# A hybrid DeltaNet / SSD decoder step: GpSimd's work between the projections moved to VectorE and ScalarE

## The chip, the cores and the metric

The kernel runs on one core of a Trainium2 chip. A core has TensorE (PE, matrix products, results in PSUM), VectorE (DVE), ScalarE (ACT), GpSimd (POOL) and SyncE (SP, which here only issues transfers). Each engine works through its own list of instructions in order and waits on semaphores for the others. The metric is the device time of one execution in microseconds; 1% of it is 28 us.

## The reference

One step of a decoder layer, for a prompt of 512 tokens and for 8 samples of 8 tokens each that continue from a state; the 576 rows are worked on together. Cut to what matters:

```
proj = rmsnorm(x) @ w_in                       # 2048 -> 6688
q, k, v = silu(causal_conv(...)); beta, g, dt from small columns
# gated delta rule, 8 heads, chunks of 64 in the reference:
low = strict(kb @ k.T * decay);  sol = solve(low + I, [v*beta, kb*exp(G)])
step: v_new = u - w @ S;  o = q_dec @ S + qk @ v_new;  S = S*g_last + k_dec.T @ v_new
o = rmsnorm(o) * silu(z)
# SSD, 2 groups of 8 heads:
step: y = (C B^T * decay) @ xdt + C_dec @ h;   h = h*a_last + (B*decay).T @ xdt
y = rmsnorm((y + D*x) * silu(z))
x = x + concat(o, y) @ w_out
x = x + (silu(rmsnorm(x) @ w_gate) * (rmsnorm(x) @ w_up)) @ w_down
y = rmsnorm(x)
```

The outputs are y for prompt and samples and the new convolution and matrix states. All of it is float32: each large product is split into a high and a low part of weights and activations and done as three matmuls.

## The kernel before, in words

There are three parts. The first (up to about 580 us) does the norm, most of the input projection and the convolutions, and leaves its results in memory (cvd, zd, gad). The third (from about 1183 us) is the rest of the output projection (`out_proj`, L1329) and the feed-forward part. The change lies in the second part, between the projections.

The second part has two kinds of work. The **chains** are `ssd(g, sd)` for two groups and `gdn(h, G)` for eight heads; each is a long line of small products, evictions and elementwise steps. A head works on four chunks of 128 columns: it builds a triangular matrix u, inverts it in blocks (16 by substitution on VectorE in t16, t16m, with a trip through memory, then 32, 64 and 128 by matmuls with the block masks bm), and then goes through the chunks (`prompt`), the samples (`sample`), the norm (`norm`) and the sample states (`states`). Heads have two sets of buffers (`slot`), so two heads are under way together. Group 0 and group 1 of the SSD run beside heads 0 to 3; each ends with a sample part that loads, scales and stores 8 states (st8, in `big`).

The **filler** are the gate projections not yet done (`gates`) and half of the output projection (`half_out`). Their matmuls write the bank pz; all other matmuls of the part write banks pm0 to pm5 (pm_5552 to pm_5557 in the order of instructions; pm_5552 and pm_5553 belong to even heads, pm_5554 and pm_5555 to odd ones). Their weights are split by ScalarE (whi) and VectorE (wlo) in pieces of 256 columns.

The order of the second part is not that of the code. The operations are noted first (L116 is the line at which a noted operation is issued, so nearly all rows of the part carry L116), with an engine, a price and what each depends on. Then `in_order` lays them out: a list scheduler that takes, over all engines, the operation that can start first by these prices, and among those the one with the longest way to the end behind it; filler matmuls come last among equals. Prices are by engine, in microseconds for n columns: VectorE's 0.07 + n / 940 for most operations, ScalarE's 0.06 or 0.085 + n / 1170, and for GpSimd

```
NPOOL = Noted("pool", nc.gpsimd, lambda op, n, ins: 0.13 + n / (300 if op == "tensor_copy" else 600))
```

The prices know nothing of one engine holding another, nor of TensorE's clock. The result is one fixed list per engine. So a change of the engine of an operation changes the order of everything behind it on all engines of this part. The third part is in an order written by hand.

GpSimd does in the second part: in `ssd` the products xdec, bex and st8 by the decay, the sum zacc and the copies eal; in `gdn` the copies egl and t16, the products of kd, q and S, the clear of ubd and the products ubd and um with the block masks.

Of the kernel before, what the change touches and what calls it, by code (L numbers as in the profile page):

```python
# [15 lines left out]
P = 128  # L16
NP = 512
NS = 64
NT = NP + NS
# [19 lines left out]
def build(tc, I, O):  # L39
    nc = tc.nc  # L40
    PE, DVE, ACT, POOL, SP = nc.tensor, nc.vector, nc.scalar, nc.gpsimd, nc.sync
    act = ACT.activation
    tt, ts, stt = DVE.tensor_tensor, DVE.tensor_scalar, DVE.scalar_tensor_tensor
    mult, add, sub, amin = ALU.mult, ALU.add, ALU.subtract, ALU.min
    with ExitStack() as ctx:
# [721 lines left out]
        def ssd(g, sd):  # L767
# [12 lines left out]
            for c in range(4):  # L780
                cc = slice(c * P, (c + 1) * P)
                for half in range(2):
                    SP.dma_start(out=ab[half], in_=gad[r0 + 4 * half:r0 + 4 * half + 4, cc].partition_broadcast(P))
                px = sbank()
                for q in range(4):
                    PE.transpose(px[:, q * P:(q + 1) * P], xs[:, q, cc], ident)
                tt(h8(xdt), h8(px), sct[:, c, 64 + 8 * g:72 + 8 * g].unsqueeze(2).broadcast_to([P, 8, 64]), mult)
                POOL.tensor_tensor(h8(xdec), h8(xdt), edl[:, c, r0:r0 + 8].unsqueeze(2).broadcast_to([P, 8, 64]), mult)
                pc = sbank()
                PE.matmul(pc[:, 0:P], bt[:, cc], ct[:, cc], start=True, stop=True)  # L790
                stt(cb, neg, 0.0, pc[:, 0:P], op0=ALU.is_ge, op1=mult)
                py = banks[5]
                for half in range(2):
                    h0 = r0 + 4 * half
                    a, d = ab[half], dec[half]
                    for j in range(4):
                        ts(d[:, j, :], a[:, j, :], sct[:, c, h0 + j:h0 + j + 1], 0.0, op0=sub, op1=amin)
                    act(d, d, AF.Exp)
                    act(a, a, AF.Exp)
                    tt(d, d, cb.unsqueeze(1).broadcast_to([P, 4, P]), mult)  # L800
                    POOL.tensor_copy(eal[:, 4 * half:4 * half + 4], a[:, :, P - 1])
                    if c:
                        tt(a, a, ct[:, cc].unsqueeze(1).broadcast_to([P, 4, P]), mult)
                    for q in range(2):
                        pr = 2 * half + q
                        for step in range(2 if c else 1):
                            for s in range(2):
                                hh, j = 2 * pr + s, 2 * q + s
                                o = py[64 * s:64 * s + 64, pr * P:(pr + 1) * P]
                                if step == 0:  # L810
                                    PE.matmul(o, h8(xdt)[:, hh, :], d[:, j, :], start=True, stop=not c)
                                else:
                                    PE.matmul(o, h8(hst)[:, hh, :], a[:, j, :], start=False, stop=True)
                pn = sbank()
                PE.matmul(pn, btok4[:, c, :], xdec, start=True, stop=True)
                for q in range(4):
                    stt(xs[:, q, cc], xs[:, q, cc], dpair[:, 4 * g + q:4 * g + q + 1], py[:, q * P:(q + 1) * P], op0=mult, op1=add)
                    new = hsts[c % 2]
                if c:
                    tt(h8(new), h8(hst), eal.unsqueeze(2).broadcast_to([P, 8, 64]), mult)  # L820
                    tt(new, new, pn, add)
                else:
                    ACT.copy(new, pn)
                hst = new
# [10 lines left out]
            for q in range(4):  # L835
                PE.transpose(px[:NS, q * P:(q + 1) * P], xs[:, q, sl], ident)
            tt(h8(xdt)[:NS], h8(px)[:NS], sct[:NS, 4, 64 + 8 * g:72 + 8 * g].unsqueeze(2).broadcast_to([NS, 8, 64]), mult)
            POOL.tensor_tensor(h8(xdec)[:NS], h8(xdt)[:NS], edl[:NS, 4, r0:r0 + 8].unsqueeze(2).broadcast_to([NS, 8, 64]), mult)
            pc = dbank()
            PE.transpose(pc[:NS, 0:P], bt[:, sl], ident)  # L840
            PE.matmul(pc[:NS, P:P + NS], bt[:, sl], ct[:, sl], start=True, stop=True)
# [1 line left out]
            ACT.copy(cbs, pc[:NS, P:P + NS])  # L843
            ACT.copy(bts, pc[:NS, 0:P])
            bex = bb[:NS, 0:8 * P].rearrange("p (a b) -> p a b", a=8)
            POOL.tensor_tensor(bex, bts.unsqueeze(1).broadcast_to([NS, 8, P]), bmask.unsqueeze(2).broadcast_to([NS, 8, P]), mult)
            ds = dec[0].rearrange("p a b -> p (a b)")[:NS].rearrange("p (a b) -> p a b", a=8)
            SP.dma_start(out=ds, in_=gad[r0:r0 + 8, sl].partition_broadcast(NS))
            for s in range(2):
# [13 lines left out]
            for q in range(4):  # L863
# [8 lines left out]
                po = dbank()  # L872
                for b in range(8):
                    PE.matmul(po[:, 8 * b:8 * b + 8], (ab[0], dec[0])[b // 4][:, b % 4, :], ct[:, NP + 8 * b:NP + 8 * b + 8], start=True, stop=True)
                POOL.tensor_tensor(st8, st8, ep[:, q, 7::8].unsqueeze(2).broadcast_to([P, 8, P]), mult)
                tt(yo, po[:, 0:NS], ep[:, q, :], mult)
                tt(xs[:, q, sl], xs[:, q, sl], yo, add)
                for half in range(2):
# [7 lines left out]
            for q in range(4):  # L886
                t = (zt, ct)[q % 2]
                SP.dma_start(out=t, in_=zd[8 + 4 * g + q])
                tt(xs[:, q], xs[:, q], t, mult)
                if q == 0:  # L890
                    act(zacc, xs[:, q], AF.Square)
                else:
                    act(t, xs[:, q], AF.Square)
                    POOL.tensor_tensor(zacc, zacc, t, add)
            ps = dbank()
            for i in range(5):
                n = P if i < 4 else NS
# [75 lines left out]
        def gdn(h, G):  # L973
# [35 lines left out]
            act(u, u, AF.Exp)  # L1009
            act(us, us, AF.Exp)  # L1010
            act(g, g, AF.Exp)
            POOL.tensor_copy(egl[:, 0:4], g[:, P - 1:NP:P])
            POOL.tensor_copy(egl[:, 4:12], g[:, NP + 7:NT:8])

            pq, pv = bank(), bank()
            for c in R4:
# [10 lines left out]
            PE.transpose(pkts[:, 0:NS], kds, ident[:NS, :NS])  # L1027
            ACT.copy(kt[:, 0:NP], pkt)
            ACT.copy(kt[:, sl], pkts[:, 0:NS])
            POOL.tensor_tensor(v4(kd), v4(kd), edl[:, 0:4, h:h + 1].broadcast_to([P, 4, P]), mult)  # L1030
            ts(kds, kds, edl[:NS, 4, h:h + 1], None, op0=mult)

            pkk, paq = bank(), bank()
# [14 lines left out]
            SP.dma_start(out=dap(ud, 0, [[P, P], [UC, 4], [1, P]]), in_=v4(u))  # L1048
            SP.dma_start(out=dap(ud, 4 * UC, [[P, NS], [1, NS]]), in_=us)
            SP.dma_start(out=u16[0:36], in_=dap(ud, 0, [[UC // 8, 36], [P, 16], [1, 16]]))  # L1050
            POOL.tensor_copy(t16, id16)
            ts(eq, eq, EPS, EPS * P, op0=add, op1=mult)
            tt(kq[:, :, 0:8], b8(kt[:, sl]), b8(g[:, sl]), mult)
            tt(kq[:, :, 8:16], b8(q[:, sl]), b8(g[:, sl]), mult)
            tt(kt[:, 0:NP], kt[:, 0:NP], g[:, 0:NP], mult)
            POOL.tensor_tensor(q[:, 0:NP], q[:, 0:NP], g[:, 0:NP], mult)
            ubd, xbd, um = (aw[:, i, 0:n].rearrange("p (a b) -> p a b", b=P) for i, n in ((0, 640), (1, 640), (2, 512)))
            POOL.memset(ubd[:, 4, :], 0.0)
            POOL.tensor_tensor(ubd[:, 0:4, :], v4(u), flat2(bm[:, 0]).unsqueeze(1).broadcast_to([P, 4, P]), mult)
            DVE.tensor_copy(ubd[:NS, 4, 0:NS], us)  # L1060
            POOL.tensor_tensor(um, v4(u), flat2(bm[:, 1]).unsqueeze(1).broadcast_to([P, 4, P]), mult)
            for i in range(15):
                m, w = 15 - i, i + 1
                pr = t16m[:36, 0:m * w].rearrange("p (a b) -> p a b", b=w)
# [73 lines left out]
            def sample():  # L1138
# [2 lines left out]
                for i in range(8):  # L1141
                    PE.matmul(pr[:, 16 * i:16 * i + 16], S[:, i, :], kq[:, i, :], start=True, stop=True)
                ACT.copy(ksq.rearrange("p a (b t) -> p b a t", t=8), pr[:, 0:P].rearrange("p (b a t) -> p b a t", a=2, t=8))
                POOL.tensor_tensor(S, S, egl[:, 4:12].unsqueeze(2).broadcast_to([P, 8, P]), mult)
                pr = bank()
                PE.transpose(pr[:NS, 0:P], ksq[:, 0, :], ident)
                tt(rs, vps, pr[:NS, 0:P], sub)
# [548 lines left out]
```

## Time and profile before

| | us |
|---|---|
| median of 3 runs | 2792.08 |
| the runs | 2801.77, 2778.82, 2792.08 |
| profiled execution, its own time | 2805.85 |
| its span, first to last instruction | 2804.1 |
| mean granted TensorE clock | 0.973 |

The page of the profile gives for each engine the busy time and its share of the span. A clock of 1.00 is TensorE's full 2.4 GHz, 0.50 is 1.2 GHz; the figure for a stretch is the mean over it. A row of the order of time gives the start, the duration, the engine, the line, the operation with what it writes and reads, its shape, and in brackets how long the engine had stood idle before it and what ended that. An instruction's duration runs from its start to its end, also where it was held in between. Matmuls overlap in part, so their durations don't add up to time. Names are those of the buffers, so that, for instance, `aw` is k, v, g, later ubd, xbd, um and S of a head, `big` holds the sample states of the SSD, and `cf` the unit matrix of a transpose.

### The profile page before, as it was taken

Reading aid. Unit: us, or ns where it says so; the run is one execution under the profiler, and the core shown is the slowest. Engines: PE = TensorE matmul, PEld = TensorE weight load, DVE = VectorE, ACT = ScalarE, POOL = GpSimd, SP = SyncE. Lnnn points to the kernel's source line nnn. Section 1 sums busy time; section 2 is a strip of 40 time slices with the busy share of each in tenths; the row PEclk is TensorE's granted clock in tenths of the full one; section 3 lists DMA queues with packets and bytes.
Section 4 is the critical chain, followed back from the end, with each engine's and each line's share of the span. In section 5 each row is a group of like instructions: output and inputs, shape, how many; then the busy total and the mean of one; then the engine's idle time right before and its main releaser. Section 6 shows DMA issues by size and latency. Waiting matters only on the chain.

```text
span 2804.1 us, 49909 instructions
## 1 busy us (share of the span) xinstructions
PE 2686.4 (96%) x19535; PEld 2583.4 (92%) x19535; DVE 2135.1 (76%) x3275; ACT 1284.7 (46%) x2441; POOL 604.0 (22%) x584
## 2 busy tenths in 40 slices
PE   7999999988998999999999999999999989999897
PEld 5999999977868898899999999999999989999896
DVE  5977888866668767588777777777777787887686
ACT  6544455542424533364443434343343455555465
POOL 1111111113122111032111010101111143343264
PEclk9999999997879999999999999999999999999999
DMA  4444444363445545464343444434343477787643
GB/s 114 118 121 116 124 124 116 114 180 107 142 128 164 170 117 151 136 196 113 98 129 109 131 115 118 128 98 128 105 132 110 137 178 191 178 189 174 161 128 133
DMA packets 580138, 380.03 MB, mean 136 GB/s; under 512 B 37022, under 2 KB 545115, under 8 KB 579326
## 3 DMA queue, kind: packets, MB, share of 16 engines
q1 hardware_dynamic: 546606, 328.91, 41.5%
q0 software_dynamic: 8384, 20.06, 4.1%
q10 hardware_dynamic: 24912, 27.88, 3.3%
q8 instruction: 153, 2.51, 0.4%
q14 instruction: 83, 0.68, 0.1%
HBM read 290.34 MB, written 86.42 MB: 134 GB/s over the span
## 4 chain that ended last, share of the span: by engine, by line
PE 52%; DVE 6%; DMA 3%; ACT 2%; issue 2%; POOL 0%; ACTq 0%; SPq 0%; DVEq 0%; POOLq 0%
PE pF L284 45%; PE pz L116 3%; PE pm L116 2%; PE pA L1329 1%; DMA wraw<-w_up 1%; DVE wlo L275 1%; DMA wraw<-w_down 1%; ACT whi L269 1%; DVE X L1301 1%; DVE ws L257 0%; DVE ws L265 0%; DMA wraw<-w_out 0%; ACT sc L1366 0%; DVE sc L1379 0%; DVE wlo L116 0%
## 5 line engine op out<-in xcount | busy, mean ns | idle before, releaser
L284 PE MATMUL pF<-X,whi 128*128 128x288 f32 x7350 | 1477.2, 297 | 25.4 <-ACT sc L1366 14.8
L284 PEld LDWEIGHTS pF<-X,whi 128*128 128x128 f32 x7350 | 1182.1, 189 | 32.9 <-ACT sc L1366 17.7
L284 PE MATMUL pF<-X,wlo 128*128 128x288 f32 x3675 | 1085.3, 295 | 0.7 <-DVE wlo L275 0.7
L284 PEld LDWEIGHTS pF<-X,wlo 128*128 128x128 f32 x3675 | 693.4, 189 | 1.6 <-DVE wlo L275 1.6
L116 PE MATMUL pF<-XR,whi 128*128 128x288 f32 (+1 forms) x2560 | 491.5, 298 | 0.6 <-DVE XR L116 0.5
L116 PEld LDWEIGHTS pF<-XR,whi 128*128 128x128 f32 (+1 forms) x2560 | 399.7, 189 | 2.6 <-DVE XR L116 1.0
L275 DVE TENSOR_TENSOR wlo<-wraw,whi 128x1024 fp32r<-128x1024 f32 (+5 forms) x285 | 355.3, 1247 | 14.4 <-ACT whi L269 13.9
L269 ACT CAST whi<-wraw 128x1024 fp32r<-128x1024 f32 (+5 forms) x285 | 266.7, 936 | 190.4 <-DVE wraw L262 66.9
L116 PE MATMUL pF<-XR,wlo 128*128 128x288 f32 (+1 forms) x1280 | 337.3, 298 | 4.0 <-DVE wlo L116 4.0
L116 ACT CAST whi<-wraw 128x256 fp32r<-128x256 f32 (+2 forms) x241 | 153.5, 643 | 270.1 <-PE pz L116 156.7
L116 PE MATMUL pz<-XR,whi 128*128 128x288 f32 x1184 | 267.7, 328 | 8.1 <-ACT zo L116 4.5
L1368 DVE TENSOR_TENSOR sc<-pF,sc 128x288 f32<-128x288 f32 x231 | 105.3, 456 | 221.8 <-PE pF L284 221.5
L269 ACT CAST whi<-ws 128x1024 fp32r<-128x1024 f32 (+5 forms) x153 | 141.4, 924 | 243.5 <-DVE ws L257 154.4
L116 PEld LDWEIGHTS pF<-XR,wlo 128*128 128x128 f32 (+1 forms) x1280 | 227.2, 189 | 5.0 <-DVE wlo L116 4.5
L116 DVE TENSOR_TENSOR wlo<-wraw,whi 128x256 fp32r<-128x256 f32 (+2 forms) x241 | 175.5, 738 | 59.9 <-PE pz L116 31.8
L116 PEld LDWEIGHTS pz<-XR,whi 128*128 128x128 f32 x1184 | 193.8, 202 | 24.2 <-issue 11.3
L1386 POOL TENSOR_TENSOR sc<-sc 128x288 f32<-128x288 f32 x22 | 37.2, 1689 | 802.6 <-DVE sc L1383 802.6
L269 ACT CAST whi<-sc 128x1024 fp32r<-128x1024 f32 (+5 forms) x101 | 89.7, 888 | 257.7 <-DVE sc L254 246.0
L1301 POOL TENSOR_TENSOR X<-X 128x288 fp32r<-128x288 f32 x140 | 146.0, 1051 | 204.3 <-ACT X L1300 176.2
L275 DVE TENSOR_TENSOR wlo<-ws,whi 128x1024 fp32r<-128x1024 f32 (+5 forms) x153 | 173.0, 1131 | 20.2 <-ACT whi L269 17.2
L1366 ACT COPY sc<-pF 128x288 f32<-128x288 f32 x308 | 121.8, 395 | 116.8 <-PE pF L284 100.5
L116 PE MATMUL pz<-XR,wlo 128*128 128x288 f32 x592 | 152.9, 327 | 0.0
(372 smaller groups left out, 3570.2 us busy)
## 6 DMA issues: line engine op xcount, KB each, us to landing
wraw<-w_in SPq DMA_DIRECT2D x104, 512.0 KB
wraw<-w_gate SPq DMA_DIRECT2D x88, 512.0 KB
wraw<-w_up SPq DMA_DIRECT2D x88, 512.0 KB
ffd<-sc SPq DMA_DIRECT2D x154, 144.0 KB
X<-ffd ACTq DMA_DIRECT2D x154, 144.0 KB
wraw<-w_down SPq DMA_DIRECT2D x45, 384.0 KB
yd<-sc POOLq DMA_DIRECT2D x26, 576.0 KB, 6.5
wraw<-w_out SPq DMA_DIRECT2D x22, 512.0 KB
```

The source lines that it names most:

```text
L116: note("dma" if op == "dma_start" else self.name, price, lambda: f(*a, **k), outs, ins, kind, op == "matmul" and not (k["start"] and k["st ...
L269: ACT.copy(hi, r)
L275: tt(lo, r, hi.bitcast(F32), sub)
L284: PE.matmul(o, a[:, k, :], b, start=k == 0 and r == 0 and q not in CHAINED, stop=k == n - 1 and r == 2, skip_group_check=q in CHAINED)
L1301: e.tensor_tensor(X[t][s][:, 1, :], raw, X[t][s][:, 0, :].bitcast(F32), sub)
L1329: PE.matmul(ps[:, l, 0:HT], w[:, kk], b[:, k, l * HT:l * HT + HT], start=k == k0 and q == 0, stop=k == 7 and q == 2)
L1366: ACT.copy(b, o)
L1368: tt(b, o, b, add)
L1386: POOL.tensor_tensor(t1, b12, b11, sub)
```

## The change

Fifteen lines in `ssd` and `gdn` name another engine. Products, sums and the clear go to VectorE (`tt` is VectorE's tensor_tensor), copies to ScalarE. Nothing else of the code changes, neither prices nor shapes. GpSimd then has nothing to do in the second part; it keeps its work in the first and third.

```diff
@@ -785,7 +785,7 @@
-                POOL.tensor_tensor(h8(xdec), h8(xdt), edl[:, c, r0:r0 + 8].unsqueeze(2).broadcast_to([P, 8, 64]), mult)
+                tt(h8(xdec), h8(xdt), edl[:, c, r0:r0 + 8].unsqueeze(2).broadcast_to([P, 8, 64]), mult)
@@ -798,7 +798,7 @@
-                    POOL.tensor_copy(eal[:, 4 * half:4 * half + 4], a[:, :, P - 1])
+                    ACT.copy(eal[:, 4 * half:4 * half + 4], a[:, :, P - 1])
@@ -835,7 +835,7 @@
-            POOL.tensor_tensor(h8(xdec)[:NS], h8(xdt)[:NS], edl[:NS, 4, r0:r0 + 8].unsqueeze(2).broadcast_to([NS, 8, 64]), mult)
+            tt(h8(xdec)[:NS], h8(xdt)[:NS], edl[:NS, 4, r0:r0 + 8].unsqueeze(2).broadcast_to([NS, 8, 64]), mult)
@@ -843,7 +843,7 @@
-            POOL.tensor_tensor(bex, bts.unsqueeze(1).broadcast_to([NS, 8, P]), bmask.unsqueeze(2).broadcast_to([NS, 8, P]), mult)
+            tt(bex, bts.unsqueeze(1).broadcast_to([NS, 8, P]), bmask.unsqueeze(2).broadcast_to([NS, 8, P]), mult)
@@ -872,7 +872,7 @@
-                POOL.tensor_tensor(st8, st8, ep[:, q, 7::8].unsqueeze(2).broadcast_to([P, 8, P]), mult)
+                tt(st8, st8, ep[:, q, 7::8].unsqueeze(2).broadcast_to([P, 8, P]), mult)
@@ -891,7 +891,7 @@
-                    POOL.tensor_tensor(zacc, zacc, t, add)
+                    tt(zacc, zacc, t, add)
@@ -1009,8 +1009,8 @@
-            POOL.tensor_copy(egl[:, 0:4], g[:, P - 1:NP:P])
-            POOL.tensor_copy(egl[:, 4:12], g[:, NP + 7:NT:8])
+            ACT.copy(egl[:, 0:4], g[:, P - 1:NP:P])
+            ACT.copy(egl[:, 4:12], g[:, NP + 7:NT:8])
@@ -1027,7 +1027,7 @@
-            POOL.tensor_tensor(v4(kd), v4(kd), edl[:, 0:4, h:h + 1].broadcast_to([P, 4, P]), mult)
+            tt(v4(kd), v4(kd), edl[:, 0:4, h:h + 1].broadcast_to([P, 4, P]), mult)
@@ -1048,17 +1048,17 @@
-            POOL.tensor_copy(t16, id16)
+            ACT.copy(t16, id16)
 ...
-            POOL.tensor_tensor(q[:, 0:NP], q[:, 0:NP], g[:, 0:NP], mult)
+            tt(q[:, 0:NP], q[:, 0:NP], g[:, 0:NP], mult)
 ...
-            POOL.memset(ubd[:, 4, :], 0.0)
-            POOL.tensor_tensor(ubd[:, 0:4, :], v4(u), flat2(bm[:, 0]).unsqueeze(1).broadcast_to([P, 4, P]), mult)
+            DVE.memset(ubd[:, 4, :], 0.0)
+            tt(ubd[:, 0:4, :], v4(u), flat2(bm[:, 0]).unsqueeze(1).broadcast_to([P, 4, P]), mult)
 ...
-            POOL.tensor_tensor(um, v4(u), flat2(bm[:, 1]).unsqueeze(1).broadcast_to([P, 4, P]), mult)
+            tt(um, v4(u), flat2(bm[:, 1]).unsqueeze(1).broadcast_to([P, 4, P]), mult)
@@ -1141,7 +1141,7 @@
-                POOL.tensor_tensor(S, S, egl[:, 4:12].unsqueeze(2).broadcast_to([P, 8, P]), mult)
+                tt(S, S, egl[:, 4:12].unsqueeze(2).broadcast_to([P, 8, P]), mult)
```

Since the orderer works with other engines and prices, the lists of all engines change in this part. Two places, as the lists stand before and after.

VectorE, in the middle of the third head (names with 5589 to 5610 are the even heads' buffers), before:

```order
L116 TENSOR_TENSOR at_5595<-pm_5553,u_5594 128x512
L116 TENSOR_SCALAR rk_5633<-rk_5633 128x5
L116 TENSOR_TENSOR kq_5610<-q_5591,aw_5589 128x8x8
L116 TENSOR_TENSOR ty_5637<-rk_5633 128x5
L116 SCALAR_TENSOR_TENSOR u_5594<-pm_5552,u_5594 128x512
L116 SCALAR_TENSOR_TENSOR ty_5637<-ty_5637,tx_5636 128x5
L116 TENSOR_TENSOR kt_5592<-kt_5592,aw_5589 128x512
```

and after:

```order
L116 TENSOR_TENSOR at_5595<-pm_5553,u_5594 128x512
L116 TENSOR_TENSOR q_5591<-q_5591,aw_5589 128x512
L116 SCALAR_TENSOR_TENSOR u_5594<-pm_5552,u_5594 128x512
L116 TENSOR_TENSOR kt_5592<-kt_5592,aw_5589 128x512
L116 TENSOR_TENSOR wlo<-wraw,whi 128x256
L116 TENSOR_TENSOR XR_94<-xs,XR_93 128x576
L116 TENSOR_TENSOR ats_5600<-pm_5552,us_5599 64x64
L116 COPY kds_5625<-pm_5555 64x128
L116 SCALAR_TENSOR_TENSOR us_5599<-pm_5552,us_5599 64x64
L116 TENSOR_TENSOR aw_5589<-u_5594,bm 128x512
L116 COPY aw_5589<-us_5599 64x64
L116 TENSOR_TENSOR aw_5589<-u_5594,bm 128x512
```

The product of q now stands between the products at and u, and the two products with the block masks stand behind the last step of us; before, these three were in GpSimd's list.

TensorE, at the end of the second part (pA is the first product of the output projection's rest), before:

```order
L116 MATMUL pm_5554<-at_5623,kds_5625 128x512
L116 MATMUL pz<-XR_93,whi 128x288
L116 MATMUL pz<-XR_94,whi 128x288 x2
L116 MATMUL pz<-XR_93,wlo 128x288 x2
...
L116 MATMUL pz<-XR_89,whi 128x288 x2
L116 MATMUL pz<-XR_88,wlo 128x288 x2
L1329 MATMUL pA<-XR_88,whi 128x288 x2
```

and after, from the last filler on:

```order
L116 MATMUL pz<-XR_88,wlo 128x288 x2
L116 MATMUL pm_5554<-vp_5624,u_5622 128x128
L116 MATMUL pm_5553<-bw_5590,kt_5592 128x128
L116 MATMUL pm_5555<-bw_5618,kd_5621 128x128
L116 MATMUL pm_5554<-bw_5618,at_5623 128x128
...
L116 MATMUL pm_5552<-at_5595,kds_5597 128x512
L116 MATMUL pm_5555<-at_5623,kds_5625 128x512
L116 MATMUL pm_5554<-at_5623,kds_5625 128x512
L1329 MATMUL pA<-XR_88,whi 128x288 x2
```

Before, fillers stand between the chains' last matmuls and behind them (167 behind the product of vp and u of the last head). After, the last filler stands just ahead of that product, and the 65 matmuls from it to the last state product follow one another with none between. The number of fillers in the part, 1776, is the same.

## Rows read from the trace of the kernel before

**Rows 1.** The page: busy time by engine; the chain that ended last.

```profile
PE 2686.4 (96%) x19535; PEld 2583.4 (92%) x19535; DVE 2135.1 (76%) x3275; ACT 1284.7 (46%) x2441; POOL 604.0 (22%) x584
...
PE 52%; DVE 6%; DMA 3%; ACT 2%; issue 2%; POOL 0%; ACTq 0%; SPq 0%; DVEq 0%; POOLq 0%
```

**Rows 2.** Busy time by stretch: length, engines' busy us (instructions), granted clock, DMA share, GB/s.

```profile
640.00:730.00 90.00, 83.68 (x403) 71.92 (x404) 53.33 (x165) 26.15 (x60) 23.96 (x21) 0.66 0.42 112
...
670.00:680.00 10.00, 10.00 (x30) 7.18 (x30) 4.92 (x27) 0.81 (x2) 0.00 (x0) 0.50 0.59 160
...
770.00:830.00 60.00, 56.37 (x288) 41.13 (x289) 38.58 (x109) 15.49 (x40) 12.99 (x11) 0.70 0.41 115
...
580.00:1190.00 610.00, 564.31 (x3811) 485.75 (x3809) 416.05 (x1285) 236.10 (x735) 113.01 (x114) 0.90 0.50 143
```

**Rows 3.** GpSimd's groups by shape, 600 to 1200: count, busy us, mean ns, idle before.

```profile
L116 POOL TENSOR_TENSOR aw<-u,bm 128x512 f32<-128x512 f32 x16 | 23.1, 1449 | 11.2 <-DVE u L116 4.2 <-DVE bts L116 2.3 <-DVE wlo L116 1.1
...
L116 POOL COPY eal<-big 128x4 f32<-128x4 f32 x7 | 3.2, 452 | 10.3 <-ACT big L116 10.3
```

**Rows 4.** VectorE's and ScalarE's nearest groups by shape, 600 to 1200.

```profile
L116 DVE TENSOR_TENSOR at<-bw,bmask 64x512 f32<-64x512 f32 x16 | 11.8, 742 | 7.2 <-PE pm L116 4.4 <-ACT bw L116 2.7
...
L116 DVE TENSOR_TENSOR big<-big,cb 128x512 f32<-128x512 f32 x7 | 4.8, 683 | 0.0
...
L116 DVE TENSOR_TENSOR xs<-xs,zt 128x576 f32<-128x576 f32 x4 | 3.0, 748 | 0.0
...
L1324 DVE TENSOR_TENSOR wlo<-wraw,whi 128x1024 fp32r<-128x1024 f32 x2 | 2.4, 1218 | 2.0 <-ACT whi L1323 2.0
...
L116 ACT COPY u<-pm 64x256 f32<-64x256 f32 x8 | 2.9, 367 | 4.6 <-DVE u L116 4.5
```

**Rows 5.** Order of time, VectorE beside GpSimd: start, us, engine, line, operation.

```profile
586.08 1.68 DVE L116 TENSOR_SCALAR dec<-ab,scr 128x128 f32<-128x128 f32 x4
...
665.92 1.91 POOL L116 TENSOR_TENSOR big<-big,zt 128x1024 f32<-128x1024 f32 x1 [3.90 <-PE pm L116]
666.01 1.89 DVE L116 TENSOR_TENSOR t16m<-u,t 36x63 f32<-36x63 f32 x1
...
667.94 0.22 DVE L116 TENSOR_TENSOR t<-t,t16m 36x63 f32<-36x63 f32 x1
...
1157.36 1.66 DVE L116 TENSOR_TENSOR at<-bw,bmask 64x512 f32<-64x512 f32 x1 [1.98 <-ACT bw L116]
```

**Rows 6.** Order of time, TensorE's gaps that VectorE ends.

```profile
588.69 2.05 PE L116 MATMUL pm<-xdec,bb 128*128 128x512 f32 x2 [1.99 <-DVE cb L116]
...
639.64 1.23 POOL L116 TENSOR_TENSOR kd<-kd,scr 128x512 f32<-128x512 f32 x1
639.88 1.06 DVE L116 TENSOR_SCALAR kds<-kds,rk 64x128 f32<-64x128 f32 x1
...
641.00 0.27 PE L116 MATMUL pm<-cf,kds 64*128 64x64 f32 x1 [1.51 <-DVE kds L116]
...
1092.81 0.24 PE L116 MATMUL pm<-cf,kds 64*128 64x64 f32 x1 [0.54 <-DVE kds L116]
```

**Rows 7.** Order of time at the end of the second part.

```profile
1137.45 0.38 PE L116 MATMUL pm<-vp,u 128*128 128x128 f32 x2
...
1171.47 0.32 SPq L116 DMA_DIRECT2D mixd<-z  x1
...
1173.55 0.43 SPq L116 DMA_DIRECT2D xs<-mixd  x1
...
1181.20 0.69 PE L116 MATMUL pz<-XR,whi 128*128 128x288 f32 x4
...
1181.40 0.76 DVE L116 TENSOR_TENSOR XR<-xs,XR 128x576 fp32r<-128x576 f32 x1
...
1181.73 0.43 PE L116 MATMUL pz<-XR,wlo 128*128 128x288 f32 x2
...
1183.09 0.77 PE L1329 MATMUL pA<-XR,whi 128*128 128x288 f32 x4 [0.94 <-DVE xs L116]
```

## The prediction

> **What bounds the kernel now.** I read the page first: its line of engine shares and its chain that ended last [rows 1]. TensorE is busy for 96% of the span, and over half of the chain that ended last is TensorE; GpSimd stands in that chain with 0%. So GpSimd sets the time only through others. Next I read the table of stretches [rows 2]. The change touches only the middle part between the two projections, which fills the window from 580 to 1190 us, 610 us of a span of 2804.1. There TensorE is busy for 564.31 us, so it idles for 45.7, and its granted clock is 0.90 of full. The clock is the larger loss: 0.10 x 610 is some 61 us. Of it 0.34 x 90 = 31 us fall between 640 and 730, and 0.30 x 60 = 18 us between 770 and 830; from 900 on the clock is 1.00. A stretch at 0.50 is the lower of the two levels, 1.2 GHz. VectorE is busy for 416 of these 610 us (68%), GpSimd for 113.
>
> Then the operations by shape, GpSimd's [rows 3] and their nearest on VectorE and ScalarE [rows 4]. A 128x512 product takes 1.45 us on GpSimd and 0.68 on VectorE; a copy of four columns takes 0.45 on GpSimd.
>
> Then the order of time where GpSimd and VectorE meet [rows 5]. At 665.92 GpSimd starts a product of 1.91 us. At 666.01 VectorE starts a 36x63 product; it takes 1.89 us, and the next one of that size takes 0.22. VectorE stood until GpSimd was through. I went through all VectorE rows of the window: 54 of them are more than 0.1 us longer than the lower quartile of their own group while GpSimd is busy, the first at 586.08 and the last at 1157.36, and what is over sums to 52.6 us.
>
> Last, TensorE's waits [rows 6]. At 641.00 it has waited 1.51 us for kds, which VectorE made in 1.06 us beside GpSimd's product from 639.64 on. Of the gaps that VectorE ends, 25 have such a held VectorE row just ahead, the first before 588.69 and the last before 1092.81. They sum to 24.9 us; counting no gap for more than its hold, 21.
>
> **VectorE's account.** The change gives VectorE, in this part, 40 products of 128x512 (16 of block masks, 8 each of q, kd and xdec), 16 of 128x1024, 6 sums of 128x576, 2 products of 64x1024, 2 of 64x512, and 8 clears. Prices from [rows 4]: 40 x 0.683 = 27.3; the nearest 128x1024 row is 1.218, so 16 and 2 of them are 21.9; 6 x 0.748 = 4.5; 2 x 0.742 = 1.5; the 128x128 clears as a quarter of a 128x512 product each, 1.4. Together 56.6 us. With no other reader on GpSimd the 52.6 us of holding go. VectorE's sum moves by +4 us, within what a stage with 194 us of idle VectorE swallows. I count it at zero. If the holding did not end, the cover would be gone and the 56.6 us would fall on an engine that the products of both chains wait for; that is a rival below. The Trainium skill, page "Perfetto Trace Analysis", section "Optimizing Scalar/DVE Operations", says that where the vector engine is saturated it can make sense to offload work to GpSimd, and it adds that between these two it may not help, as they share a read port. Its first half speaks against this change, and by it VectorE would carry 56.6 us more; by its second half, and by the held rows here, only 4.
>
> **ScalarE's copies.** 32 copies of four or eight columns and 8 of 40x256 go to ScalarE. Its nearest row, 64x256 in 0.367 us, bounds all 40 at 14.7 us, on an engine busy for 236 of 610. What they could hold up is what stands behind one that waits: the 40x256 copy waits until a transfer has read its old values. The weight splits stand behind it, and TensorE's next filler matmuls behind them. I take zero, since ScalarE idles for 374 us; up to 5 us on the slow side (8 copies at less than one microsecond) stay in the range.
>
> **TensorE's gaps.** What follows a moved operation on VectorE's own queue no longer waits on another engine, and the orderer now counts the work on the engine on which it costs. But VectorE's sum is unchanged, so a needed operation can still stand behind a moved one, at about half the length that GpSimd's had (0.68 against 1.45). Bounds: 0 and -24.9 us. I take half of the 24.9, **-12 us**.
>
> **The clock.** It falls where small matmuls with gaps between them come together: in 640 to 730 and 770 to 830, the two places where the sample part of an SSD group runs beside two heads, with gaps such as that at 641.00. Fewer gaps can keep it up. Bounds: all of the 49 us come back, or 15 more are lost (a third such stretch like 770 to 830). From 670 to 680 TensorE is granted 0.50 while it never idles, so the gaps are not all of it. I take a quarter, **-12 us**.
>
> **The tail.** The order of instructions has a term against the change. The filler matmuls (pz: gate projections and half of the output projection) are 1776 in both kernels. Before, 167 of them stand behind the head chains' last product with an inverted block (vp by u of the last head), and the filler ends last [rows 7]: that product starts at 1137.45, the last filler at 1181.73, and the output projection at 1183.09. After, the last filler stands ahead of that product, and 65 matmuls of the chains follow alone. Before, these 45.6 us hold 167 x 0.132 = 22 us of filler (four fillers from 1181.20, the next at 1181.73), so the chains' own matmuls take at most 23.6, and every wait of the chain was filled. After, the 22 us of filler have run earlier, in what would be gaps, and the waits of the tail are bare: three rounds of product, difference, product, copy, product per chunk, the sample part, the norm, and then the way of the last head's output through memory, from the store's issue at 1171.47 to the split at 1181.40. Of that way about 5 us are needed: 2.1 from the store's issue to the load's, the same again for the load as an estimate, and 0.76 for the split. Bounds: 5 us (only that way is bare) and 21 (the chain takes the 45.6 us that it took beside the filler). I take **+12 us**, about the middle.
>
> **The sum.** -12 - 12 + 12 = -12 us against the profiled execution's own 2805.85, so 2794. That execution is 13.8 us above the median of the runs shown, 2792.08; I take the difference from the median: **2780 us**. Its own range is 2760 to 2806. About 1% (28 us) is what a measurement of this kernel can tell from no change.
>
> **Rivals.**
> - The clock stays up. If most low stretches at the SSD groups hang on the held VectorE rows, 40 of the 49 us come back, with the gaps at -14 and the tail at +12: 2792 - 42 = 2750. For it: the gap of 1.51 us at 641.00, behind a held row, stands just where the first low stretch begins [rows 2, 6]. Against it: the level stays at 0.50 where TensorE has no gap at all. Chance 0.25.
> - The filler runs out too soon, the rival on the other side. It decides at the point where the last pz matmul ends before the head chains do: the tail then takes the full +21, the output projection and the tail's matmuls begin at the lower level (half speed over some 15 us of work, +7), and the gaps stay: +28, so 2820. For it: the order of instructions, in which the filler is ahead of the chains from the first heads on (1043 pz stand before the first state product of the third head, before 864). Against it: filler that runs earlier fills gaps. Chance 0.15.
> - VectorE becomes the bound: the 56.6 us come and the holds do not go, or what goes was not in the way. By the ratio of now, 24.9 us of gaps for 52.6 of holding, 56.6 more would make 27 us of gaps; with the tail's 12, +39, so 2831. This is what the first half of the Trainium skill's rule on offloading would give; the held rows speak against it. Chance 0.06.
> - The forecast, 0.54.
>
> **Chances and range.** Faster by over 1% (under 2764): the first rival and a little of the forecast's lower end, 0.27. Slower by over 1% (over 2820): half of the second and third rivals and a little for copies and clock together, 0.15. Within 1%: 0.58. The range takes in the first rival's time and ten us below it, and the second rival's with six above; outside it are the third rival and the outer ends of the first two, some 0.2: 2740 to 2826.
>
> **What would show it.** Right: no VectorE row of the window held to GpSimd's length (the 36x63 products at 0.22 throughout); VectorE's busy time there within 10 us of 416; TensorE's gaps ended by VectorE under 27 us ahead of the tail; the last pz matmul some 20 us or more ahead of the output projection, with TensorE idle for about 12 us between. Wrong: the granted clock under 0.86 over the part (more low stretches), a tail without idle time, VectorE's busy time above 450, or ScalarE's splits waiting behind the 40x256 copies.

## The result: 1.2% faster, inside the range, and by more clock than forecast

The changed kernel takes 2761.19 us (median of 4 runs, 2755.85 to 2767.53) against 2796.93 for the kernel before (4 runs): a ratio of 0.9878, 95% interval 0.9829 to 0.9928. Run again beside the experiments it gave 0.9849 (0.9815 to 0.9882) and 0.9886 (0.9839 to 0.9932). That is 19 us below the forecast of 2780, just past the 1% bound, and 11 us above the first rival (2750). The change from one kernel to the other is 36 us where the sum had 12; it lies inside the range because the range was 86 us wide. The profiled execution's own time is 2767.53, 38.3 below that of before. The ratios leave out executions more than 1.5% above the fastest of their kernel, which drops 7 of the 29 executions of the kernel before that stand beside e8 to e10 and after_third, and no other.

The page of the kernel after, its shares and the chain that ended last, which answers to [rows 1], with the row of the granted clock in 40 slices:

```profile
PE 2657.0 (96%) x19535; PEld 2557.9 (92%) x19535; DVE 2129.7 (77%) x3349; ACT 1293.0 (47%) x2483; POOL 490.9 (18%) x470
PEclk9999999999999999899999999999999999999998
PE 63%; DVE 5%; issue 3%; DMA 2%; ACT 2%; POOL 1%; ACTq 0%; SPq 0%; DVEq 0%; POOLq 0%
```

GpSimd has lost its work of the second part, and VectorE's busy time has hardly moved. The stretches of [rows 2] in the kernel after, then the whole second part (first pz to first pA) and its tail (last pz to first pA). Columns: stretch, its length, busy time (and instructions) of PE, PEld, DVE, ACT and POOL, the granted clock, DMA's share, GB/s:

```profile
640.00:730.00 90.00, 86.57 (x556) 72.73 (x555) 70.01 (x232) 38.75 (x94) 0.00 (x0) 0.89 0.55 160
670.00:680.00 10.00, 9.94 (x64) 7.66 (x63) 8.98 (x37) 3.83 (x6) 0.00 (x0) 1.00 0.43 124
770.00:830.00 60.00, 58.68 (x376) 47.34 (x377) 40.95 (x128) 28.06 (x87) 0.00 (x0) 0.97 0.62 186
570.04:1141.10 571.06, 536.99 (x3818) 460.81 (x3818) 409.29 (x1360) 244.62 (x780) 0.00 (x0) 0.95 0.53 153
1109.84:1141.10 31.26, 25.42 (x121) 15.73 (x119) 19.88 (x61) 7.95 (x40) 0.00 (x0) 0.75 0.33 99
```

The same part before:

```profile
572.32:1183.09 610.77, 565.40 (x3818) 487.07 (x3819) 415.19 (x1286) 236.28 (x737) 113.01 (x114) 0.90 0.49 142
```

It went from 610.8 to 571.1 us, by 39.7; that is the whole difference. With the same 3818 matmuls TensorE is busy for 28.4 us less, at a mean clock of 0.95 for 0.90, and it idles for 11.3 us less (45.4 to 34.1 by these two rows). By the order of time the idle time ahead of the tail fell from 44.3 to 28.1 (VectorE's share 35.8 to 21.9), and the tail's rose from 0.9 to 5.7.

### The profile page after: what moved, and what is told of

Same layout as the page of the kernel before. It is cut to its first block, busy times and chain, and to the rows that moved or that the text cites. A ratio compares the mean times of both kernels' runs of the same rounds, so it can differ in the third digit from the quotient of the medians.

```text
span 2765.7 us, 49762 instructions
## 1 busy us (share of the span) xinstructions
PE 2657.0 (96%) x19535; PEld 2557.9 (92%) x19535; DVE 2129.7 (77%) x3349; ACT 1293.0 (47%) x2483; POOL 490.9 (18%) x470
## 4 chain that ended last, share of the span: by engine, by line
PE 63%; DVE 5%; issue 3%; DMA 2%; ACT 2%; POOL 1%; ACTq 0%; SPq 0%; DVEq 0%; POOLq 0%
PE pF L284 47%; PE pm L116 7%; PE pz L116 7%; PE pA L1329 2%; DMA wraw<-w_up 1%; DVE wlo L275 1%; DVE X L1301 1%; ACT whi L269 1%; ACT jk L116 0%; POOL X L1301 0%; DMA wraw<-w_down 0%; DVE xs L116 0%; DMA bw<-tid 0%; DMA wraw<-w_out 0%; DVE ws L257 0%
## 5 line engine op out<-in xcount | busy, mean ns | idle before, releaser
L116 PE MATMUL pz<-XR,whi 128*128 128x288 f32 x1184 | 249.2, 316 | 4.9 <-DVE xs L116 2.4
L116 PEld LDWEIGHTS pz<-XR,whi 128*128 128x128 f32 x1184 | 184.1, 194 | 15.4 <-issue 5.6
L116 DVE TENSOR_TENSOR wlo<-wraw,whi 128x256 fp32r<-128x256 f32 (+2 forms) x241 | 168.4, 712 | 29.7 <-ACT whi L116 14.7
L116 PE MATMUL pz<-XR,wlo 128*128 128x288 f32 x592 | 146.7, 314 | 0.0
```

Of the source, the lines that this page charges most:

```text
L116: note("dma" if op == "dma_start" else self.name, price, lambda: f(*a, **k), outs, ins, kind, op == "matmul" and not (k["start"] and k["st ...
```

## The rows that were moved

VectorE's and ScalarE's forms in the second part of the kernel after (form, count, busy us, mean ns of one, idle before). They answer to [rows 3, 4]:

```profile
L116 DVE TENSOR_TENSOR aw<-u,bm 128x512 f32<-128x512 f32 x16 | 10.8, 680 | 0.0
L116 DVE TENSOR_TENSOR aw<-aw,egl 128x1024 f32<-128x1024 f32 x8 | 9.8, 1221 | 6.2 <-PE pm L116 3.7 <-DMA q<-cvd 2.4
L116 DVE TENSOR_TENSOR kd<-kd,rk 128x512 f32<-128x512 f32 x8 | 5.5, 687 | 0.1
L116 DVE TENSOR_TENSOR t<-t,t16m 36x63 f32<-36x63 f32 x16 | 3.4, 213 | 0.2
L116 DVE TENSOR_SCALAR kds<-kds,rk 64x128 f32<-64x128 f32 x8 | 2.2, 272 | 0.0
L116 ACT COPY t<-id 40x256 f32<-40x256 f32 x8 | 3.2, 404 | 0.6 <-DMA tid<-t 0.6
```

and the kernel before, for three forms that had been held:

```profile
L116 DVE TENSOR_TENSOR kd<-kd,rk 128x512 f32<-128x512 f32 x8 | 8.3, 1035 | 0.3
L116 DVE TENSOR_TENSOR t<-t,t16m 36x63 f32<-36x63 f32 x16 | 5.1, 316 | 0.4
L116 DVE TENSOR_SCALAR kds<-kds,rk 64x128 f32<-64x128 f32 x8 | 4.6, 576 | 0.0
```

The first row is a moved product: 0.680 us, for which the sum had 0.683. The next is a moved product of 1024 columns, 1.221 for 1.218. No row of VectorE's in the second part is held any more: the 36x63 products all stand near 0.21, where one in [rows 5] had taken 1.89. The moved operations sum to 56.4 us and 52.6 us of holding went; by the sum of its instructions' durations VectorE went from 475.2 to 478.6 us. Its busy time, which counts once where two instructions overlap, went from 415.2 to 409.3.

The tail, which answers to [rows 7]: TensorE's rows, then SyncE's and VectorE's for the last head's output (start, duration, engine, line, operation, count, and in brackets the idle time and what ended it).

```profile
1109.33 0.51 PE L116 MATMUL pz<-XR,wlo 128*128 128x288 f32 x2
1109.68 0.38 PE L116 MATMUL pm<-vp,u 128*128 128x128 f32 x2
1121.43 1.96 PE L116 MATMUL pm<-kq,aw 128*128 128x16 f32 x16
1128.58 1.12 PE L116 MATMUL pm<-cf,vp 128*128 128x128 f32 x4 [2.03 <-DVE vp L116]
1133.76 3.72 PE L116 MATMUL pm<-at,kds 64*128 64x512 f32 x4
1138.25 2.07 PE L116 MATMUL pm<-at,kds 64*128 64x512 f32 x2 [0.78 <-DVE at L116]
1141.10 1.33 PE L1329 MATMUL pA<-XR,whi 128*128 128x288 f32 x4 [0.78 <-DVE aw L116]
```

```profile
1134.82 0.32 SPq L116 DMA_DIRECT2D mixd<-z  x1
1139.29 0.75 SPq L116 DMA_DIRECT2D xs<-mixd  x1
1144.80 0.76 DVE L116 TENSOR_TENSOR XR<-xs,XR 128x576 fp32r<-128x576 f32 x1 [1.42 <-ACT XR L116]
```

The last filler stands ahead of the last head's product vp by u, as the list said, and 31.3 us follow without filler. But TensorE is busy for 25.4 of them, where the prediction allowed the chains' matmuls at most 23.6; the clock falls to 0.75 there, which costs some 7.8 us by estimate (0.25 x 31.3). Only 5.7 us are idle. The way of the last head's output through memory, which the prediction took as a bare wait, is not waited for: the products of the states (at by kds) run beside it, and the output projection begins at 1141.10, 3.7 us ahead of the last split at 1144.80.

## Experiments

All ratios are to executions of the kernel before on the same chip, beside the experiment: e1 to e4 share one chip, after_again and e5 to e7 a second, e8 to e10 and after_third a third, and over the executions that the ratios use the kernel before has a median there of 2787.1, 2799.5 and 2793.0. So medians are compared within one of these groups. The table has, for each kernel's profile, the second part from the first pz to the first pA: its length, TensorE's busy time, its idle time, the mean granted clock, and the time by which VectorE's rows were held (what they took over the lower quartile of their form while GpSimd was busy).

| kernel | median us | ratio (95%) | part | busy | idle | clock | held |
|---|---|---|---|---|---|---|---|
| before (profile ahead) | 2796.93 | 1 | 610.8 | 565.4 | 45 | 0.90 | 52.6 |
| after | 2761.19 | 0.9878 (0.9829 to 0.9928) | 571.1 | 537.0 | 34 | 0.95 | 0 |
| after_again | 2759.73 | 0.9849 (0.9815 to 0.9882) | 560.6 | 529.1 | 32 | 0.97 | 0 |
| after_third | 2758.40 | 0.9886 (0.9839 to 0.9932) | 561.0 | 528.8 | 32 | 0.97 | 0 |
| e1, after's order, on GpSimd | 2767.56 | 0.9914 (0.9872 to 0.9956) | 594.2 | 555.7 | 39 | 0.92 | 45.2 |
| e2, before's order, on VectorE | 2773.68 | 0.9926 (0.9890 to 0.9962) | 572.7 | 538.9 | 34 | 0.95 | 0 |
| e3, products alone | 2769.69 | 0.9909 (0.9877 to 0.9942) | 577.9 | 540.5 | 37 | 0.93 | 0 |
| e4, copies alone | 2793.72 | 1.0007 (0.9973 to 1.0041) | 612.0 | 569.4 | 43 | 0.90 | 50.3 |
| e5, two units held back | 2768.59 | 0.9872 (0.9841 to 0.9904) | 576.6 | 536.1 | 40 | 0.95 | 0 |
| e6, before, paced | 2812.69 | 1.0027 (1.0002 to 1.0053) | 623.4 | 572.3 | 51 | 0.89 | 45.7 |
| e7, after, paced | 2785.90 | 0.9950 (0.9926 to 0.9974) | 591.4 | 549.8 | 42 | 0.93 | 0 |
| e8, dummy products | 2789.09 | 0.9989 (0.9959 to 1.0020) | 592.1 | 546.0 | 46 | 0.93 | 34.7 |
| e9, after, filler later | 2780.21 | 0.9951 (0.9921 to 0.9980) | 590.3 | 552.6 | 38 | 0.92 | 0 |
| e10, before, filler earlier | 2773.50 | 0.9945 (0.9913 to 0.9978) | 578.0 | 530.8 | 47 | 0.97 | 51.1 |

One profile is one execution, and executions of one program differ: e1's profile took 2785.17, 18 us above e1's median. The mean granted clock is known for every execution, so the clock can also be told from all of them. Lost to the clock is here (1 - clock) x span, an estimate that takes TensorE as busy throughout; the rest is the time without it. For 75 executions of the kernel before the time has a standard deviation of 11.4 us and the rest one of 3.7. Means over the executions that the ratios use:

| kernel | lost to the clock | the rest |
|---|---|---|
| before, three chips | 66.6, 71.0, 66.8 | 2726.5, 2728.0, 2725.3 |
| after, after_again, after_third | 44.9, 48.8, 45.5 | 2716.6, 2712.6, 2715.0 |
| e1, after's order, on GpSimd | 56.0 | 2714.8 |
| e2, before's order, on VectorE | 57.7 | 2715.7 |
| e4, copies alone | 64.8 | 2727.8 |
| e5, two units held back | 49.3 | 2718.8 |
| e8, dummy products | 64.9 | 2726.1 |
| e9, after, filler later | 70.2 | 2709.7 |
| e10, before, filler earlier | 45.8 | 2728.7 |

The change is worth some 12 us of the rest and 21 us of the clock.

**Place and order apart (e1, e2).** The change does two things: it names another engine, and by that moves the orderer's lists. e1 keeps the lists of the kernel after and runs the moved operations on GpSimd; e2 keeps the lists of before and runs them on VectorE and ScalarE.

```diff
 # e1
+PD, PA = Noted("dve", nc.gpsimd, NDVE.price), Noted("act", nc.gpsimd, NACT.price)
-tt(v4(kd), ...)                  # and so at each moved product and copy
+PD.tensor_tensor(v4(kd), ...)
 # e2
+VD = Noted("pool", nc.vector, NPOOL.price)
-POOL.tensor_tensor(v4(kd), ...)
+VD.tensor_tensor(v4(kd), ...)
```

> The order of all engines that the change makes, but the moved operations still run on GpSimd (same places in time, TensorE's list identical to that of the changed kernel). Theory 'held rows' (the gain comes from VectorE no longer standing while GpSimd reads, and from the low clock that follows TensorE's gaps): no gain, ratio to before 1.00 to 1.01, and rows of VectorE held to GpSimd's length again. Rival 'order' (the gain comes from the new order of instructions, whichever engine runs the moved ones): ratio 0.985 to 0.992 as for the change.

> The order of before on all engines (TensorE's list identical to before), but VectorE and ScalarE run the moved operations. Theory 'held rows': at least the gain of the change, ratio 0.978 to 0.988, since filler is also left for the end of the part and the bare tail goes. Rival 'order': ratio 0.997 to 1.003; VectorE gets 57 us more work at places that were not planned for it, so even slower is possible under it.

Each alone gives under 1%: 0.9914 for the order, 0.9926 for the place; their product, 0.984, is about what both give. By these ratios the order is worth as much as the place, and I had priced it as a loss (the tail) and nothing else. e1 fell where its rival was, e2 between its two theories. In e2 all holding is gone and the idle time falls from 45 to 34 in before's own order; in e1 the holding stays at 45.2, and the rest falls as far. So either alone brings nearly all of the 12 us of the rest and about half of the clock's 21; together they add up in the clock alone.

**Products and copies apart (e3, e4).** e3 leaves the copies on GpSimd, e4 moves the copies alone.

```diff
 # e3: as after, but
-ACT.copy(eal[...], ...); ACT.copy(egl[...], ...); ACT.copy(t16, id16)
+POOL.tensor_copy(eal[...], ...); POOL.tensor_copy(egl[...], ...); POOL.tensor_copy(t16, id16)
 # e4: as before, but
-POOL.tensor_copy(eal[...], ...); POOL.tensor_copy(egl[...], ...); POOL.tensor_copy(t16, id16)
+ACT.copy(eal[...], ...); ACT.copy(egl[...], ...); ACT.copy(t16, id16)
```

> Products, sums and the clear to VectorE as in the change; the 40 small copies stay on GpSimd. Theory 'held rows': nearly the whole gain, ratio 0.985 to 0.992, since the copies are 11 us of GpSimd's 113 in the part and hold little. Rival 'copies' (the wait for a second engine at the small copies was what cost): ratio 0.995 to 1.00.

> Only the 40 small copies go to ScalarE; products, sums and the clear stay on GpSimd. Theory 'held rows': no difference, ratio 0.997 to 1.003, VectorE rows still held. Rival 'copies': ratio 0.988 to 0.995.

The copies alone are worth nothing (1.0007), as priced. The copies that GpSimd keeps in e3 take 14.9 us, for which I had 11, and hold next to nothing (two VectorE rows, 0.3 us together). e3 gives 0.9909, in the range of 'held rows'; its interval overlaps with that of the whole change.

**The tail and the slack (after_again, e5, e6, e7).** e5 makes the last two units of the filler wait in the plan for the last heads' chunks, which fills the tail; e6 and e7 raise VectorE's prices in the plan of the second part by 12%, to see whether the order helps by leaving room for what holds VectorE.

```diff
 # e5
-filler(lambda: half_out(QS))
+filler(lambda: half_out(QS[:-2]))
+# the matmuls of the last two units depend on heads 6 and 7 having their inverse
 # e6 (before) and e7 (after)
-NDVE = Noted("dve", nc.vector, lambda op, n, ins: 0.13 + ...)
+NDVE = Noted("dve", nc.vector, lambda op, n, ins: 1.12 * (0.13 + ...))   # second part
```

> The changed kernel once more, beside the others of this call on one chip, so that they can be compared with it. Ratio to before 0.985 to 0.993.

> The changed kernel, with the matmuls of the last two filler units (144 of 1776) held in the plan until heads 6 and 7 begin their chunks, so that filler stands in the tail (111 behind the last head's vp by u instead of none). In the changed kernel's trace the tail from the last filler to the output projection is 31.3 us, with 5.7 us of idle TensorE and a clock of 0.75 (7.8 us). Theory 'bare tail costs': 5 to 13 us faster than the changed kernel, ratio to it 0.995 to 0.998, no low clock at the end. Rival 'the heads' chain sets the end, and filler in the tail only slows it': same or slower than the changed kernel.

> The kernel before, every operation on the engine where it was, but the plan of this part counts VectorE's operations 1.12 times as long (by about what holding adds). Filler is then placed earlier (1320 of 1776 ahead of the chains' 1000th matmul, before 1248, the change 1386). Theory 'slack in the order' (the order of the change gains since its plan gives VectorE more time, so that TensorE has filler where VectorE is late): ratio to before 0.989 to 0.995, as the order of the change had with GpSimd. Rival 'the order's gain came from where the moved operations stand': ratio 0.998 to 1.003.

> The changed kernel with the same 1.12 on VectorE's prices: still more filler early, a longer bare tail. Theory 'slack in the order': fewer gaps ahead of the tail (28 us in the changed kernel, here 18 to 25), but a tail some 5 us longer, so within 0.997 to 1.003 of the changed kernel. Rival 'more slack is always better': 5 us or more faster than the changed kernel.

In e5 the tail is 1.5 us long in place of 31.7, and the kernel is not faster but, by the medians, 9 us slower than after_again (the intervals of the two ratios overlap): ahead of the tail TensorE now idles for 39.0 us in place of 26.2. The filled tail was paid for ahead of it. e6 and e7 are slower than the kernels that they change, by 0.3 and 1.0%, and e7 lies outside both ranges given for it: the slack theory falls.

**Holding alone, and where the filler stands (e8, e9, e10).** e8 puts idle work back on GpSimd in the kernel after, and nothing else. e9 and e10 change one number, the threshold under which the orderer puts filler ahead of a chain matmul.

```diff
 # e8, behind each moved product of 128x512 and twice behind each of 128x1024
+nc.gpsimd.tensor_tensor(out=spare, in0=x, in1=x, op=mult)   # two halves of 128x256; nobody reads spare
 # e9 (after)
-in_order(near=0.1, far=0.28, warm=1.0)
+in_order(near=0.1, far=0.28, warm=0.9)
 # e10 (before)
-in_order(near=0.1, far=0.28, warm=1.0)
+in_order(near=0.1, far=0.28, warm=1.1)
```

> The kernel after, with idle work put back on GpSimd alone: 144 products of 128x256 that read what a moved product has just written (or a table beside it) and write into unused columns. TensorE's, VectorE's and ScalarE's lists are those of the kernel after; nothing of the reference is left out. Holding theory (VectorE's rows stand while GpSimd makes a product): held rows come back, some 40 us or more of them, VectorE's gaps on TensorE rise from 21.9 to 27 us or more, and the kernel loses what separates the run with after's order on GpSimd from the kernel after: 0.4 to 0.8% slower than the kernel after of this call, a ratio of 0.990 to 0.995. Rival (what the moved products cost on GpSimd was their own 1.45 us and the wait across engines): held rows come back, but the ratio stays that of the kernel after, 0.984 to 0.988.

> The kernel after, with the orderer's threshold below which it puts filler ahead of a chain matmul lowered from 1.0 to 0.9: 1259 becomes 1315 filler matmuls ahead of the eighth tenth of the chains' (1400 in the kernel after), and 9 chain matmuls in place of 66 behind the last filler. Tail theory (the bare tail costs what I priced, some 12 us, and filler used early isn't missed there): the tail falls from 31 us to under 5, the other gaps rise by less than 6, and the kernel is 6 to 12 us faster than the kernel after, a ratio of 0.981 to 0.984. Exchange theory (filler only moves gaps; the order of the kernel after helps because its filler comes earlier): gaps ahead of the tail rise by about what the tail loses, as where the last two units were held back, and the time is within 0.3% of the kernel after or up to 10 us slower, 0.985 to 0.990.

> The kernel before, with the same threshold raised from 1.0 to 1.1: filler comes earlier, 1300 filler matmuls ahead of the eighth tenth of the chains' in place of 1259, in 377 pieces in place of 358, with 8 chain matmuls behind the last. All products stay on GpSimd. If the order of the kernel after helps because filler comes earlier and in places where TensorE has been little used: the clock of the part rises from 0.90 to 0.92 or more and the ratio is 0.990 to 0.995. If it helps for another reason (the places of the moved products themselves in VectorE's list): 0.998 to 1.003.

> The kernel after again, as the base of this call: 0.984 to 0.989 of the kernel before; a granted clock of 0.95 or more in the part between the projections, a tail of about 31 us.

**e8** is the strongest of the set: 2789.09 against 2758.40 for the kernel after beside it on the same chip, 30.7 us, with the same lists on TensorE, VectorE and ScalarE and with every real product on VectorE. It is more than either theory said. By the profiles TensorE idles for 46 us in place of 32 (+14) and is busy for 546.0 in place of 528.8 (+17); over all executions the rest grows by 11 us and the clock's loss by 19. In e8's profile no wait of TensorE, VectorE or ScalarE in the part is ended by GpSimd, so waits across engines are not what it costs. The second part of e8 and of after_third, columns as above:

```profile
570.69:1162.81 592.12, 546.04 (x3819) 470.06 (x3819) 444.77 (x1360) 244.22 (x779) 120.89 (x144) 0.93 0.51 147
571.61:1132.64 561.03, 528.77 (x3819) 453.73 (x3819) 408.68 (x1360) 245.01 (x780) 0.00 (x0) 0.97 0.54 156
```

GpSimd's and VectorE's rows at one place in e8:

```profile
675.41 2.06 POOL L965 TENSOR_TENSOR scr<-aw 128x256 bf16<-128x256 f32 x3
677.56 3.02 POOL L965 TENSOR_TENSOR scr<-zt 128x256 bf16<-128x256 f32 x4
```

```profile
676.89 0.66 DVE L116 TENSOR_TENSOR t<-t,t16m 36x55 f32<-36x55 f32 x1
677.58 0.66 DVE L116 TENSOR_TENSOR t16m<-u,t 36x60 f32<-36x60 f32 x1
678.27 0.66 DVE L116 TENSOR_TENSOR t<-t,t16m 36x60 f32<-36x60 f32 x1
```

A 36x60 product of 0.21 us takes 0.66, the length of one dummy (2.06 / 3 = 0.69). This is also the third rival of the prediction made real: 56.6 us of products on VectorE, and the holding still there. VectorE is busy for 444.8 us, and the kernel is back at the time of before (0.9989). That is more than the holding costs in the change itself: e1, with the same lists, 45.2 us of holding and the products on GpSimd, keeps a ratio of 0.9914, so holding is worth there what separates e1 from the kernel after, some 0.3 to 0.7% (on different chips). The Trainium skill, "SBUF — State Buffer", says in its section "SBUF: two separate sides" that VectorE and GpSimd share a pair of ports, which a GpSimd instruction or a VectorE instruction with two inputs in SBUF (or in a mode of two ports) has for its whole length while the other stands still. The rows agree, down to products of 36 partitions. A row with one tensor input was held too: kds in [rows 6] took 1.06 us, and takes 0.27 in the kernel after. No run tells whether it works in a mode of two ports.

**e9** has a tail of 10.4 us in place of 31.3 and is 21.8 us slower than after_third: TensorE idles 5 us more in all and is busy 24 us longer. The tail theory falls, and the exchange theory, which had at most 10 us, does not give the size either: over all executions the rest is 5 us lower than after_third's and the clock's loss 25 us higher. **e10** leaves every product on GpSimd, with 51.1 us of holding and as much idle time as before, and is faster by 0.55% with the clock at 0.97, as its first theory had it; its gain is the clock alone (21 us less lost, the rest 3 us longer). A stretch of e9 and two of e10, columns as above:

```profile
760.00:770.00 10.00, 10.00 (x40) 8.45 (x39) 4.02 (x5) 1.44 (x4) 0.00 (x0) 0.50 0.36 105
```

```profile
640.00:730.00 90.00, 83.46 (x542) 72.49 (x543) 67.76 (x204) 36.04 (x88) 23.96 (x21) 0.89 0.55 159
770.00:830.00 60.00, 55.57 (x378) 43.48 (x376) 45.93 (x126) 28.28 (x85) 22.05 (x16) 1.00 0.69 198
```

In e9 the clock stands at 0.50 from 760 to 800 with TensorE never idle; in e10 the second low place of [rows 2] is gone (1.00 where before had 0.70) and the first is at 0.89 for 0.66. None of the ten variants beats the kernel after.

## Why the prediction was right, and where not

- **What bounds it: right.** TensorE's idle time and low clock in the second part, and nothing outside it, hold the whole difference.
- **VectorE's account, 0 taken: right.** Busy time within 6 us of before, the moved operations' sum within 1% (56.4 for 56.6), no held row left. e8 shows that with the products on VectorE and the holding still there the gain is gone. The third rival had put 27 us of gaps on that; e8 has 14 us more of gaps that VectorE ends than after_third (33.6 and 19.7), and what remains of its 30.7 us is clock, which the rival left out.
- **ScalarE's copies, 0 taken: right** (e4, 1.0007). All 40 sum to 9.7 us, under the 14.7 of the sum. The eight 40x256 copies take 0.404 us each, for which it had 0.367, and ScalarE idles ahead of all eight for 0.6 us, so they hold up the splits behind them for no longer.
- **TensorE's gaps, -12 taken: about right.** Ahead of the tail -16.2; VectorE's share of them -13.9, and e8 gives +14 back with the holding. But the end of the holding was not needed for them: in e1's profile, with 45.2 us of holding, VectorE's gaps ahead of the tail are 24.2 us, 11.6 under before's. The sum tied them to the held rows alone.
- **The tail, +12 taken: right in size by luck, wrong in kind.** It measured 4.8 us more idle time and 7.8 us of low clock, 12.6. I had 12 us of idle time, some 5 of them for the last head's output on its way through memory, on which the output projection's start does not wait. And neither try had the cost back: e5 and e9 shorten the tail to 1.5 and 10.4 us and are slower.
- **The clock, -12 taken: this is the step that was mis-sized.** By the two profiles the clock ahead of the tail gave back some 36 us (TensorE's busy time fell by 28.4 in the part, and 7.8 that the tail lost come on top). Over all executions the whole kernel loses 21 us less to the clock, the tail's loss included, so some 29 ahead of it. "Bounds: all of the 49 us come back" was the end it was near. I weighted it at a quarter because the stretch 670 to 680 stood at 0.50 without a gap. That row says only that the gap need not lie in the stretch; it says nothing about what brought the level down. Two sources were there: the held rows (e2, which keeps before's order, loses 9 us less to the clock) and the order itself, which I had charged for the tail and credited with nothing (e1, with the holding left, loses 11 us less; e10 21).
- **The rivals.** The first (clock stays up, 2750, chance 0.25) came nearer than the forecast (11 us off against 19), and its mechanism is what came, though not by the held rows alone. The second (filler runs out too soon, 2820) met its condition, last pz ahead of the end of the chains by 31 us, and its sign was wrong: the order with the early filler (e1) is faster than before, tail and all.
- **Against which time.** The profile of before, 2805.85, is itself 9 us above the median of its four runs, so the 38 us between the profiles are somewhat more than the 36 between the medians, and more than the 33 between the means over the executions that the ratios use.

What stays open is which feature of the order keeps the clock up. Two numbers of each list do not tell it: within the first eight tenths of the chains' matmuls stand 1259 filler matmuls before, 1300 in e10 (faster), 1336 in e6 (slower), 1400 in the kernel after; 358 pieces of filler before, 377 in e10 (faster), 382 in e4 (the same).

## What to carry to other kernels

Before work goes to GpSimd beside a busy VectorE, look for VectorE rows that are longer than their own form elsewhere: here 113 us of GpSimd work held VectorE for 53, nearly what the work costs on VectorE itself. Where an orderer with fixed prices lays the lists, a change of engine is two changes, and each must be priced with both signs; run one with the other's lists to tell them apart. A bare stretch at the end is not by itself a loss: what fills it has been taken from somewhere. And where the clock moves from one execution to the next, read it over many executions before a single profile is believed.

## What the runs showed of the hardware that was not expected

The same lists give another clock from one execution to the next. The stretch from 640 to 650 and the same four products in the kernel after:

```profile
640.00:650.00 10.00, 10.00 (x39) 8.20 (x39) 5.62 (x24) 5.65 (x21) 0.00 (x0) 0.53 0.09 21
638.89 0.33 PE L116 MATMUL pm<-dec,xdt 64*64 64x64 f32 x4 [0.57 <-DVE xs L116]
647.87 3.78 PE L116 MATMUL pm<-bb,xdec 64*128 64x512 f32 x4
```

and in after_third, the same kernel:

```profile
640.00:650.00 10.00, 9.36 (x71) 7.26 (x70) 8.82 (x33) 6.29 (x23) 0.00 (x0) 1.00 0.16 50
641.52 0.33 PE L116 MATMUL pm<-dec,xdt 64*64 64x64 f32 x4 [0.58 <-DVE xs L116]
647.23 1.98 PE L116 MATMUL pm<-bb,xdec 64*128 64x512 f32 x4
```

The wait just ahead is the same (0.57 and 0.58), and the products take 3.78 us at the lower level and 1.98 at the full one. Over the three profiles of this kernel the part takes 571.1, 560.6 and 561.0 us, with idle times of 34, 32 and 32: nearly all of the 10 us between executions is the clock. The kernel before varies more: the 75 executions of it that the ratios use run from 2765.64 us at a mean clock of 0.985 to 2819.42 at 0.968.

GpSimd is held in turn. In e8, while VectorE was busy without a break (7.00 us of the stretch 626 to 633), two dummy products that take 1.44 us elsewhere took 5.72:

```profile
586.22 1.44 POOL L965 TENSOR_TENSOR scr<-xdec 128x256 bf16<-128x256 f32 x2 [36.50 <-DMA cneg<-c_n]
626.65 5.72 POOL L965 TENSOR_TENSOR scr<-xdec 128x256 bf16<-128x256 f32 x2 [12.89 <-DVE xdec L116]
```
